# A decoder step on one core: sample state by 32 rows, masked queries against streamed states, and the memory rows of both layers split ahead on VectorE

## The chip, the cores and the metric

The kernel runs on one core of a Trainium2 chip. The time is device microseconds from the first to the last instruction with what the runtime adds around them; the median of several runs counts. The engines are TensorE (PE; its weight loads are shown as PEld), VectorE (DVE), ScalarE (ACT), GpSimd (POOL), and SyncE (SP), which here issues most of the DMAs.

## The reference, cut to what matters

Two layers of a decoder. Layer 0 mixes tokens with HGRN2, a gated linear recurrence with a matrix state of 128 x 128 for each of 8 heads; layer 1 with RWKV-7. Both add a cross attention of 4 heads to a memory of 256 rows, a gate and an output projection. There is one prompt of 1024 tokens from a zero state, and a sample group of 8 sequences with 8 tokens each, which start from given states. What the change touches is the memory's keys and values and the sample group's part of HGRN2:

```python
def memory_kv(mem, g, w):
    kv = rmsnorm(mem, g) @ w
    k, v = jnp.split(kv, 2, axis=-1)
...
    b = jnp.cumsum(gc, axis=2)
    o = jnp.einsum('bhts,bhse->bhte', att, vc) + jnp.einsum('bhtd,bhde->bhte', qc * jnp.exp(b), S)
    b_last = b[:, :, -1:, :]
    S = jnp.exp(b_last[:, :, 0, :])[..., None] * S + jnp.einsum('bhsd,bhse->bhde', kc * jnp.exp(b_last - b), vc)
```

For each head and each of the 8 sequences the output is a product inside the 8 tokens plus decayed queries times the old state; the new state is the decayed old one plus decayed keys times values.

## The kernel before

Everything is fp32. Large products are made of three products of halves: an operand is split into a high part (rounded to fp32r by ACT, "whi", "memh") and a low part (what is left, "wlo", "meml", by POOL or DVE), in `split` (L197 to L200); `mm3` (L216 to L218) adds high x high, high x low and low x high. Small products are plain fp32, and one of them shows as two MATMUL and two weight loads in the trace.

Layer 0 goes through these stages: the tokens are normed and transposed; the values of all heads are made and stored ("vtk"); `memory_kv` makes the memory's keys and values of both layers; then come the eight heads, with the cross attention and the gates as filling between them (the table FILL); then the output projection. Layer 1 follows.

`memory_kv` norms the 256 memory rows once. For each layer it then transposes them on PE (L290), multiplies by the layer's gain on DVE (L291) and splits them into memh and meml, of which there is one buffer each. Eight weight blocks of 128 columns are loaded by SP (L209), split (the low part on POOL for even, on DVE for odd blocks) and multiplied with the rows, 24 matmuls a block; keys and values are transposed back and stored (L311 to L316).

`hgrn_head` makes queries and decays of one head for the 1024 + 64 tokens and calls `hgrn_half` twice; the second call has the sample group's 64 tokens, 8 for each sequence, behind its 512. At its end (from L738 on) it reads the 8 old states of the head in two tiles S0 of four (in the trace, where buffer numbers are left out, S0 is S), and makes

- pi (L744): for each sequence, the state as weights and its 8 queries streamed, which gives the output transposed; ACT copies it to oi (L747);
- pos (L749, L750): the product inside the tokens, plus oi times the identity, which turns it back; then the norm and a transpose into oT;
- kts, the keys transposed (L753, L755), and for each tile of four sequences vx (L758), the values masked by sequence with `blk`, decayed states (L760), the product pds of all 64 keys' rows with vx (L762), the sum (L763) and a store by POOL (L764).

pi, pos, the transposes and pds take turns in two PSUM banks ("z"); vx has one buffer.

The order of the instructions on each engine isn't the program's. The kernel is built with `schedule_with_timeline_sim=True`: a planner plays the program through with times of its own and gives each engine, out of what would be ready, what stands first in the program. So work of different heads, gates and attention is mixed on each engine, and an engine then takes its work strictly in the planned order. Tiles lie in pools that are stacked from both ends of the on-chip memory; with `reuse_waits="tile"` a tile waits only for those tiles that lay at its addresses before.

Of the kernel before, what the change touches and what calls it, by code (L numbers as in the profile page):

```python
# [9 lines left out]
F32 = mybir.dt.float32  # L10
F32R = mybir.dt.float32r
# [43 lines left out]
BF = dict(hs=3, oT=3, qk=3, zn=3, lt=4, kb=2, tot=2, vv=3, cmp=2, kt=1, S=6, oi=1, kts=1, S0=2, vx=1)  # L55
# [94 lines left out]
def pool(g, name, bufs, side="left"):  # L150
    return g.tc.tile_pool(name=name, bufs=bufs, side=side, reuse_waits="tile")
# [117 lines left out]
def memory_kv(g, mp, sp, kT0, v0):  # L269
# [6 lines left out]
    for i in range(2):  # L276
        x = sp("mx")[:, :D]
        nc.sync.dma_start(out=x, in_=g.mem_prompt[0, 128 * i:128 * i + 128, :])
        norm_rows(g, xs[i], x, 128)
    for layer in range(2):  # L280
        mh = mp.tile([128, KT, MEM], F32R, name="memh", tag="memh", bufs=1)
        ml = mp.tile([128, KT, MEM], F32R, name="meml", tag="meml", bufs=1)
        gb = g.vec[:, g.vo["mg"] + layer * KT:g.vo["mg"] + (layer + 1) * KT]
        for i in range(2):
            h = sp("mx")[:, :D].rearrange("p (k t) -> p k t", t=128)
            for b in range(2):
                ps = g.psm.tile([128, 4, 128], F32, name="pt", tag="m")
                for j in range(4):
                    k = 4 * b + j
                    nc.tensor.transpose(ps[:, j, :], xs[i][:, 128 * k:128 * k + 128], g.ident)  # L290
                nc.vector.tensor_tensor(h[:, 4 * b:4 * b + 4], ps, gb[:, 4 * b:4 * b + 4, None].to_broadcast([128, 4, 128]),  # L291
                                        op=ALU.mult)
            sl = (slice(None), slice(None), slice(128 * i, 128 * i + 128))
            split(g, mh[sl], ml[sl], h)
# [6 lines left out]
        for j in range(8):  # L301
            w = load_w(g, mp, g.w_mem_kv[layer, :, 128 * j:128 * j + 128], 128, elo="dve" if j % 2 else "pool", raws=3)
# [128 lines left out]
def hgrn_masks(g, c):  # L431
    nc = g.nc
    si = c.tile([128, 32], I32, name="si")
    ti = c.tile([128, 32], I32, name="ti")
    xi = c.tile([128, 32], I32, name="xi")
# [4 lines left out]
    a = c.tile([128, 32], F32, name="ma")  # L440
    b = c.tile([128, 32], F32, name="mb")
    u = c.tile([128, 32], F32, name="mu_")
# [5 lines left out]
    for n, h in enumerate((2, 4, 8, 16)):  # L448
# [3 lines left out]
        nc.vector.tensor_mul(lev[:, n, :], a, u)  # L452
    return base, lev
# [17 lines left out]
def hgrn_layer(ctx, g):  # L471
# [29 lines left out]
    with pool(g, "xk", 1, "right") as xk:  # L501
# [7 lines left out]
        with pool(g, "hm", 1, "right") as hm, pool(g, "h2", 1, "right") as h2, pool(g, "xc", 1, "right") as xc, \  # L509
# [3 lines left out]
            mbase, mlev = hgrn_masks(g, hm)  # L513
# [107 lines left out]
def hgrn_half(g, hd, half, h2, own, mbase, mlev, qk, zn, lt, vv, att, atts, oT, S):  # L621
# [115 lines left out]
    pi = g.ph["z"].tile([128, TS], F32, name="pi", tag="m")  # L737
    S0 = []  # L738
    for j in range(2):
        s0 = mt("S0", 4, 128)  # L740
        nc.sync.dma_start(out=s0, in_=g.state_hgrn[0, 4 * j:4 * j + 4, hd].rearrange("b d e -> d b e"))
        for b in range(4):
            o = LS * (4 * j + b)
            nc.tensor.matmul(pi[:, o:o + LS], s0[:, b, :], qe[:, 512 + o:512 + o + LS], start=True, stop=True)  # L744
# [4 lines left out]
    nc.tensor.matmul(po[:, 0, :], atts, vv[:64, 4], start=True, stop=False)  # L749
    nc.tensor.matmul(po[:, 0, :], oi, g.ident, start=False, stop=True)  # L750
# [5 lines left out]
    for j, s0 in enumerate(S0):  # L756
        vx = mt("vx", 4, 128, p=64)
        nc.vector.tensor_tensor(vx, vv[:64, 4:5].to_broadcast([64, 4, 128]),  # L758
                                g.blk[:64, 4 * j:4 * j + 4, None].to_broadcast([64, 4, 128]), op=ALU.mult)
        nc.vector.tensor_tensor(s0, s0, ebs[:, 4 * j:4 * j + 4, None].to_broadcast([128, 4, 128]), op=ALU.mult)  # L760
        pd = g.ph["z"].tile([128, 4, 128], F32, name="pds", tag="m")
        nc.tensor.matmul(pd, kt, vx, start=True, stop=True)  # L762
# [1090 lines left out]
```

## Time and profile before

| | |
|---|---|
| median of 3 runs | 2398.97 us (2397.93 to 2401.8) |
| the profiled execution | 2401.76 us, its span 2399.8 us |
| PE busy | 2238.2 us, 93% of the span |
| DVE, ACT, POOL busy | 1332.2, 1004.3, 717.7 us |
| mean clock granted to PE | 0.934 of full speed |

In a row of the windows stand the stretch, its length, for each engine the busy time and in brackets the number of instructions, then the clock granted to PE (1.00 is full speed), the busy share of the DMA engines and GB/s. In a row of the timeline stand the start, the time that it took, the engine, the line, the operation, output and input, shapes and count, and in square brackets how long the engine stood idle before it and for what. Matmuls are pipelined, so the distance of two starts, not the duration of one, is what a matmul costs. In a row of groups stand the count, the busy time in us, the mean of one in ns, and the idle time ahead.

### The profile page before, as it was taken

The numbers are of one execution on the slowest core, as the hardware profiler recorded it, in microseconds if no ns is written. First come the engines' busy times: TensorE is split into PE (matmuls) and PEld (weight loads), VectorE is DVE, ScalarE is ACT, GpSimd is POOL, SyncE is SP. The second block draws the span as 40 slices with busy tenths as digits, with TensorE's granted clock in tenths as the row PEclk, the third lists the DMA queues.
The fourth block names the chain that finished last, engine by engine and source line by source line (L and its number), as shares of the span: only waits on it lengthen the run. The fifth ranks groups of instructions, "written<-read, shape, count | busy, mean of one in ns | idle before, by whom it ended". The sixth has DMA issues, their size and how long they took to land. (4 is left out here: it accounts for less than half of the span.)

```text
span 2399.8 us, 50625 instructions
## 1 busy us (share of the span) xinstructions
PE 2238.2 (93%) x20980; PEld 2001.5 (83%) x20981; DVE 1332.2 (56%) x2678; ACT 1004.3 (42%) x2240; POOL 717.7 (30%) x559
## 2 busy tenths in 40 slices
PE   5988999999999979989989998999999998899997
PEld 5988888888788858878979998898889987788786
DVE  6113566556775553365796214245576589874643
ACT  4222444444444442266554313344544455444421
POOL 2123121122112310034553412113143255444432
PEclk9998999999999989999999998999986798887999
DMA  5334111223432264215434425145332233312653
GB/s 184 86 96 142 48 56 45 67 70 91 111 87 87 80 193 127 84 41 199 148 122 163 127 93 145 50 103 134 113 108 72 57 101 99 90 55 82 201 158 105
DMA packets 360312, 252.99 MB, mean 105 GB/s; under 512 B 120379, under 2 KB 326403, under 8 KB 360083
## 3 DMA queue, kind: packets, MB, share of 16 engines
q1 hardware_dynamic: 348034, 237.66, 33.3%
q0 software_dynamic: 2544, 7.64, 0.9%
q10 hardware_dynamic: 9504, 4.46, 0.7%
q8 instruction: 165, 2.70, 0.5%
q14 instruction: 65, 0.52, 0.1%
HBM read 172.59 MB, written 77.11 MB: 104 GB/s over the span
## 5 line engine op out<-in xcount | busy, mean ns | idle before, releaser
L200 POOL TENSOR_TENSOR wlo<-wraw,whi 128x1024 fp32r<-128x1024 f32 (+1 forms) x84 | 214.9, 2560 | 646.5 <-ACT whi L197 623.8
L216 PE MATMUL pg<-hi,whi 128*128 128x288 f32 (+3 forms) x800 | 269.1, 336 | 4.5 <-DVE qk L597 2.3
L218 PE MATMUL pg<-hi,wlo 128*128 128x288 f32 (+3 forms) x800 | 266.0, 333 | 0.0
L217 PE MATMUL pg<-lo,whi 128*128 128x288 f32 (+3 forms) x800 | 265.9, 332 | 0.0
L197 ACT ACTIVATE whi<-wraw 128x1024 fp32r<-128x1024 f32 (+1 forms) x92 | 101.0, 1099 | 178.5 <-issue 104.9
L216 PEld LDWEIGHTS pg<-hi,whi 128*128 128x128 f32 x800 | 153.8, 192 | 21.5 <-issue 4.4
L217 PEld LDWEIGHTS pg<-lo,whi 128*128 128x128 f32 x800 | 153.7, 192 | 12.9 <-issue 3.1
L218 PEld LDWEIGHTS pg<-hi,wlo 128*128 128x128 f32 x800 | 153.5, 192 | 11.8 <-issue 2.3
L890 PE MATMUL pout<-owh,bh 128*128 128x512 f32 (+1 forms) x432 | 143.1, 397 | 9.2 <-ACT owh L197 9.2
L890 PE MATMUL pout<-owl,bh 128*128 128x512 f32 (+1 forms) x432 | 142.0, 394 | 0.1
L890 PE MATMUL pout<-owh,bl 128*128 128x512 f32 (+1 forms) x432 | 141.2, 394 | 0.9 <-DVE bl L200 0.9
L216 PE MATMUL pg<-xhi,whi 128*128 128x384 f32 (+2 forms) x392 | 127.6, 325 | 7.1 <-DVE evs L1136 5.0
L218 PE MATMUL pg<-xhi,wlo 128*128 128x384 f32 (+2 forms) x392 | 126.4, 322 | 0.0
L217 PE MATMUL pg<-xlo,whi 128*128 128x384 f32 (+2 forms) x392 | 125.5, 320 | 0.0
L1461 PE MATMUL psc<-AR,BKz 128*128 128x128 f32 x544 | 98.2, 342 | 17.2 <-DVE Q L1464 9.3
L1461 PEld LDWEIGHTS psc<-AR,BKz 128*128 128x128 f32 x544 | 86.7, 244 | 23.1 <-DVE Q L1464 11.0
L890 PEld LDWEIGHTS pout<-owh,bh 128*128 128x128 f32 (+1 forms) x432 | 78.9, 183 | 31.3 <-ACT owh L197 10.8
L197 ACT ACTIVATE bh<-br 128x512 fp32r<-128x512 f32 (+1 forms) x54 | 32.4, 606 | 171.5 <-POOL br L859 84.4
L200 DVE TENSOR_TENSOR bl<-br,bh 128x512 fp32r<-128x512 f32 (+1 forms) x54 | 49.6, 919 | 96.2 <-ACT bh L197 96.2
L890 PEld LDWEIGHTS pout<-owh,bl 128*128 128x128 f32 (+1 forms) x432 | 78.6, 182 | 22.8 <-DVE bl L200 1.8
L242 PE MATMUL pg<-xhi,wlo 128*128 128x384 f32 (+1 forms) x408 | 96.6, 334 | 0.0
L890 PEld LDWEIGHTS pout<-owl,bh 128*128 128x128 f32 (+1 forms) x432 | 78.8, 183 | 21.1 <-DVE owl L200 0.6
(460 smaller groups left out, 6114.9 us busy)
## 6 DMA issues: line engine op xcount, KB each, us to landing
wraw<-in_w_in_dram SPq DMA_DIRECT2D x72, 512.0 KB
oraw<-in_w_out_dram SPq DMA_DIRECT2D x24, 512.0 KB
wraw<-in_w_mem_kv_dram SPq DMA_DIRECT2D x16, 512.0 KB
gT<-evs SPq DMA_DIRECT2D x12, 544.0 KB
vv<-vtk SPq DMA_DIRECT2D x24, 256.0 KB
br<-brT SPq DMA_DIRECT2D x24, 256.0 KB
br<-mixT SPq DMA_DIRECT2D x24, 256.0 KB
gt<-gT SPq DMA_DIRECT2D x24, 256.0 KB
```

The costliest lines, as they stand in the source:

```text
L197: nc.scalar.activation(hi, src, AF.Copy)
L200: (nc.gpsimd if elo == "pool" else nc.vector).tensor_sub(lo, src, hi.bitcast(F32))
L216: nc.tensor.matmul(out, ah, bh, start=first, stop=False)
L217: nc.tensor.matmul(out, ah, bl, start=False, stop=False)
L218: nc.tensor.matmul(out, al, bh, start=False, stop=last)
L242: nc.tensor.matmul(z[:, :n], a[:, k], x(k)[:, t0:t0 + n], start=first, stop=last)
L890: nc.tensor.matmul(ps[c][:p], a[:, k, :p], w[:, 512 * c:512 * c + 512], start=first, stop=last)
L1461: nc.tensor.matmul(ps[:, j], two(BK[:, h, j, 2 * e:2 * e + 2]), two(AR[:, j, 2 * e:2 * e + 2]), start=True, stop=True)
```

## The change

In `memory_kv` a first loop over the two layers makes the transposes, the gain and the split for both, with two buffers each for memh and meml, the low parts on DVE; a second loop makes the products, with the low parts of all weights on DVE.

In `hgrn_half` the 64 queries are copied four times, each copy masked to one sequence in four ("qm", with a new mask `cmask` that `hgrn_masks` makes). The output of the old states is then made in place: for each of the four sequences of a tile, 32 masked queries are the weights and the state is streamed (128 columns), added onto 32 rows of pos; the first tile gives rows 0 to 31, the second rows 32 to 63. pi, oi, ACT's copy and the product with the identity go. For the new states the values are masked once for all 64 rows, four ways (with `bmask`, row modulo 32), and each tile's product takes 32 rows of keys and of vx; both products are made ahead of the decays and sums. The pool of masks moves to the left side, and its temporaries to a pool of their own that closes at once.

```diff
-BF = dict(..., S=6, oi=1, kts=1, S0=2, vx=1)
+BF = dict(..., S=6, qm=1, kts=1, S0=2, vx=1)
...
+    ops = []
     for layer in range(2):
-        mh = mp.tile([128, KT, MEM], F32R, name="memh", tag="memh", bufs=1)
-        ml = mp.tile([128, KT, MEM], F32R, name="meml", tag="meml", bufs=1)
+        mh = mp.tile([128, KT, MEM], F32R, name="memh", tag="memh", bufs=2)
+        ml = mp.tile([128, KT, MEM], F32R, name="meml", tag="meml", bufs=2)
...
-            split(g, mh[sl], ml[sl], h)
+            split(g, mh[sl], ml[sl], h, elo="dve")
+        ops.append((mh, ml))
+    for layer in range(2):
+        mh, ml = ops[layer]
...
-            w = load_w(..., 128, elo="dve" if j % 2 else "pool", raws=3)
+            w = load_w(..., 128, elo="dve", raws=3)
...
+    ci, cb = (tmp.tile([128, 4, 64], I32, name=nm) for nm in ("ci", "cb"))
+    nc.gpsimd.iota(ci, pattern=[[0, 4], [1, 64]], base=0, channel_multiplier=0)
+    nc.gpsimd.iota(cb, pattern=[[1, 4], [0, 64]], base=0, channel_multiplier=0)
+    nc.vector.tensor_scalar(ci, ci, 31, 3, op0=ALU.bitwise_and, op1=ALU.logical_shift_right)
+    g.cmask = c.tile([128, 4, 64], F32, name="cmask")
+    nc.vector.tensor_tensor(g.cmask, ci, cb, op=ALU.is_equal)
...
-        with pool(g, "hm", 1, "right") as hm, pool(g, "h2", 1, "right") as h2, ...
+        hm = es.enter_context(pool(g, "hm", 1))
+        with pool(g, "hmt", 1, "right") as tmp:
+            mbase, mlev = hgrn_masks(g, hm, tmp)
+        with pool(g, "h2", 1, "right") as h2, ...
...
-    pi = g.ph["z"].tile([128, TS], F32, name="pi", tag="m")
-    S0 = []
+    qm = mt("qm", 4, TS)
+    nc.vector.tensor_tensor(qm, qe[:, None, 512:].to_broadcast([128, 4, TS]), g.cmask, op=ALU.mult)
+    po = g.ph["z"].tile([64, 1, 128], F32, name="pos", tag="m")
+    nc.tensor.matmul(po[:, 0, :], atts, vv[:64, 4], start=True, stop=False)
+    S0, rs = [], [slice(32 * j, 32 * j + 32) for j in range(2)]
     for j in range(2):
         s0 = mt("S0", 4, 128)
         nc.sync.dma_start(out=s0, in_=g.state_hgrn[...])
-        for b in range(4):
-            o = LS * (4 * j + b)
-            nc.tensor.matmul(pi[:, o:o + LS], s0[:, b, :], qe[:, 512 + o:512 + o + LS], start=True, stop=True)
         S0.append(s0)
-    oi = mt("oi", TS)
-    nc.scalar.activation(oi, pi, AF.Copy)
-    po = g.ph["z"].tile([64, 1, 128], F32, name="pos", tag="m")
-    nc.tensor.matmul(po[:, 0, :], atts, vv[:64, 4], start=True, stop=False)
-    nc.tensor.matmul(po[:, 0, :], oi, g.ident, start=False, stop=True)
+    for b in range(4):
+        for r, s0 in zip(rs, S0):
+            nc.tensor.matmul(po[r, 0, :], qm[:, b, r], s0[:, b, :], start=False, stop=b == 3)
...
-    for j, s0 in enumerate(S0):
-        vx = mt("vx", 4, 128, p=64)
-        nc.vector.tensor_tensor(vx, vv[:64, 4:5].to_broadcast([64, 4, 128]),
-                                g.blk[:64, 4 * j:4 * j + 4, None].to_broadcast([64, 4, 128]), op=ALU.mult)
+    vx = mt("vx", 4, 128, p=64)
+    nc.vector.tensor_tensor(vx, vv[:64, 4:5].to_broadcast([64, 4, 128]),
+                            g.bmask[:64, :4, None].to_broadcast([64, 4, 128]), op=ALU.mult)
+    pds = [g.ph["z"].tile([128, 4, 128], F32, name="pds", tag="m") for _ in range(2)]
+    for r, pd in zip(rs, pds):
+        nc.tensor.matmul(pd, kt[r], vx[r], start=True, stop=True)
+    for j, (s0, pd) in enumerate(zip(S0, pds)):
         nc.vector.tensor_tensor(s0, s0, ebs[:, 4 * j:4 * j + 4, None]..., op=ALU.mult)
-        pd = g.ph["z"].tile([128, 4, 128], F32, name="pds", tag="m")
-        nc.tensor.matmul(pd, kt, vx, start=True, stop=True)
         nc.vector.tensor_add(s0, s0, pd)
```

More of the change, by code (lines that the diff above doesn't have):

```diff
@@ L54 @@
 RB1 = dict(s=5, AR=6, Q=6, BKt=5, BKts=2, UV=3, UVs=2, XN=1, XP=1, W=3, S0=2, S1=2, yv=3, o4=3, ec=6, ecs=2, Sn0=2)
-BF = dict(hs=3, oT=3, qk=3, zn=3, lt=4, kb=2, tot=2, vv=3, cmp=2, kt=1, S=6, oi=1, kts=1, S0=2, vx=1)
+BF = dict(hs=3, oT=3, qk=3, zn=3, lt=4, kb=2, tot=2, vv=3, cmp=2, kt=1, S=6, qm=1, kts=1, S0=2, vx=1)
 QW = 640
@@ L301, in memory_kv @@
         for j in range(8):
-            w = load_w(g, mp, g.w_mem_kv[layer, :, 128 * j:128 * j + 128], 128, elo="dve" if j % 2 else "pool", raws=3)
+            w = load_w(g, mp, g.w_mem_kv[layer, :, 128 * j:128 * j + 128], 128, elo="dve", raws=3)
             dst = kT[:, j, :] if j < 4 else vT[:, j - 4, :]
@@ L428, in sample, with hgrn_masks @@
             nc.sync.dma_start(out=g.mixT[D:, TP:].rearrange("(h c) t -> c h t", c=128), in_=self.os)
-def hgrn_masks(g, c):
+def hgrn_masks(g, c, tmp):
     nc = g.nc
-    si = c.tile([128, 32], I32, name="si")
-    ti = c.tile([128, 32], I32, name="ti")
-    xi = c.tile([128, 32], I32, name="xi")
+    si = tmp.tile([128, 32], I32, name="si")
+    ti = tmp.tile([128, 32], I32, name="ti")
+    xi = tmp.tile([128, 32], I32, name="xi")
     nc.gpsimd.iota(si, pattern=[[0, 32]], base=0, channel_multiplier=1)
@@ L439, in hgrn_masks @@
     nc.vector.tensor_tensor(xi, si, ti, op=ALU.bitwise_xor)
-    a = c.tile([128, 32], F32, name="ma")
-    b = c.tile([128, 32], F32, name="mb")
-    u = c.tile([128, 32], F32, name="mu_")
+    a = tmp.tile([128, 32], F32, name="ma")
+    b = tmp.tile([128, 32], F32, name="mb")
+    u = tmp.tile([128, 32], F32, name="mu_")
     nc.vector.tensor_tensor(u, ti, si, op=ALU.is_ge)
@@ L508, in hgrn_layer @@
         g.ph = {k: ph.get(k, ph["o"]) for k in "loz"}
-        with pool(g, "hm", 1, "right") as hm, pool(g, "h2", 1, "right") as h2, pool(g, "xc", 1, "right") as xc, \
+        hm = es.enter_context(pool(g, "hm", 1))
+        with pool(g, "hmt", 1, "right") as tmp:
+            mbase, mlev = hgrn_masks(g, hm, tmp)
+        with pool(g, "h2", 1, "right") as h2, pool(g, "xc", 1, "right") as xc, \
                 pool(g, "hq", 1, "right") as hq, pool(g, "hs", BF["hs"], "right") as hs:
@@ L512, in hgrn_layer @@
             hslot = lambda nm, b=0: hs.tile([128, 1024], F32, name=nm, tag="s")
-            mbase, mlev = hgrn_masks(g, hm)
             att = [hm.tile([128, 4, 128], F32, name=f"att{j}") for j in range(2)]
```

## The prediction

> **What bounds the kernel now.** I read the table of windows first, to see which engine fills which stage, then the timeline of PE where it isn't full.
>
> ```profile
> span 2399.8 us, 50625 instructions
> ...
> core 0: us, PE busy (x) PEld busy (x) DVE busy (x) ACT busy (x) POOL busy (x), PEclk, DMA share, GB/s
> 149.00:225.00 76.00, 61.00 (x448) 58.02 (x446) 20.86 (x26) 25.85 (x37) 31.79 (x20) 0.87 0.48 140
> 260.00:845.00 585.00, 577.21 (x6208) 490.04 (x6207) 363.95 (x930) 266.61 (x658) 122.35 (x97) 0.98 0.26 75
> 1620.00:2230.00 610.00, 573.58 (x8153) 524.21 (x8151) 415.23 (x796) 285.21 (x700) 253.93 (x256) 0.84 0.34 92
> ```
>
> The memory stage (149 to 225) has PE idle for 15 of 76 us and a clock of 0.87. The heads (260 to 845) have PE busy for 577.2 of 585 us at a clock of 0.98, while DVE, the next engine, has 364. So in the heads time taken off PE is time taken off the span, and in the memory stage PE's gaps have to be looked at.
>
> ```profile
> 149.05 1.91 PE L290 MATMUL pt<-ident,mxs 128*128 128x128 f32 x16
> 156.09 0.58 PE L216 MATMUL pg<-memh,whi 128*128 128x256 f32 x1 [5.13 <-ACT whi L197]
> ...
> 160.38 0.58 PE L218 MATMUL pg<-memh,wlo 128*128 128x256 f32 x1 [1.55 <-DVE wlo L200]
> ...
> 189.26 0.27 PE L290 MATMUL pt<-ident,mxs 128*128 128x128 f32 x1
> ...
> 192.62 0.80 PE L216 MATMUL pg<-memh,whi 128*128 128x256 f32 x2 [1.45 <-ACT memh L197]
> 196.98 0.58 PE L217 MATMUL pg<-meml,whi 128*128 128x256 f32 x1 [3.57 <-POOL meml L200]
> ...
> 202.43 0.28 PE L216 MATMUL pg<-memh,whi 128*128 128x256 f32 x1
> 202.55 0.28 PE L217 MATMUL pg<-meml,whi 128*128 128x256 f32 x1
> ...
> 189.30:202.40 13.10, 7.11 (x34) 6.34 (x32) 3.11 (x4) 3.49 (x5) 5.91 (x5) 0.61 0.38 120
> ```
>
> There are two gaps. The first opens when the transposes of layer 0's memory rows end, and PE waits for the first weights: for their high part till 156.09, for a low part till 160.38. The second stands between the layers: memh and meml exist once, so layer 1's rows can be split only after layer 0's last product, and PE waits for memh (ACT) and then for meml (POOL). The clock granted in the second is 0.61, since the idle time slows what follows.
>
> **Memory, second gap.** From 189.26 to 202.43 are 13.2 us, and they hold 34 matmuls. At the full pitch of 0.12 us (202.43 to 202.55) these need 4.1 us, so the gap with its slow clock costs 9.1 us. With two buffers each, layer 1's memh and meml are ready some 30 us earlier, and the products of layer 1 follow those of layer 0; what is late next there is the weights, whose path (load, ACT, split) already keeps step inside a layer. I take 9.0 off.
>
> **Memory, what moves to the front.** The 16 transposes of layer 1 go from among the products to the first gap. Sixteen of them are 1.91 us at 149.05, a pitch of 0.11, so 1.8 us leave a stretch where PE is full, and the new place lies inside PE's idle 5.13 us. With them go four mults by the gain, and all meml and all weight splits go from POOL to DVE:
>
> ```profile
> L291 DVE TENSOR_TENSOR mx<-pt,vec 128x512 f32<-128x512 f32 x8 | 5.1, 684 | 71.9 <-PE pt L290 71.9
> ...
> L200 DVE TENSOR_TENSOR wlo<-wraw,whi 128x1024 fp32r<-128x1024 f32 x8 | 11.0, 1380 | 41.5 <-ACT whi L197 41.5
> ...
> L200 POOL TENSOR_TENSOR meml<-mx,memh 128x1024 fp32r<-128x1024 f32 x4 | 9.4, 2350 | 49.8 <-ACT memh L197 49.8
> ```
>
> DVE gets 8 more weight splits and 4 rows of meml, 12 x 1.38 = 16.6 us, on top of its 20.9 in this stage: 37 of some 65 us, so it isn't the bound. A layer's product of 24 matmuls takes 24 x 0.12 = 2.9 us and its weight split 1.4, so the splits keep pace, and a low part is there 1 us sooner than from POOL (2.35 for the same shape). The question is the order on DVE in the first gap. If the planner puts all of layer 1's rows ahead of the first weight split, DVE has 8 x 0.68 + 4 x 1.38 + 1.38 = 12.3 us to do from about 149.5 on (four transposes after 149.05), and the first low weights come at 161.8 instead of 160.38, with those of the next product 1.4 us behind: up to 2 us lost. If the split of the weights goes between them, it ends at about 157.5 (PE starts on the high part at 156.09, and 1.38 behind that): 3 us won. I take zero, and keep +2 and -3.
>
> **Masks and addresses.** The batch mask adds two DVE operations of 256 elements and two iotas to the masks, which end just ahead of the first evacuation of head 0:
>
> ```profile
> 232.05 0.20 DVE L452 TENSOR_TENSOR mlev<-ma,mu__2183 128x32 int32<-128x32 f32 x1
> 232.16 0.68 DVE L157 TENSOR_SCALAR qk<-pg 128x512 f32<-128x512 f32 x1
> ...
> 236.50 0.61 PE L216 MATMUL pg<-hi,whi 128*128 128x288 f32 x1 [2.34 <-DVE qk L597]
> ```
>
> That evacuation starts as soon as DVE is through with the masks, and PE waits for what follows from it. At 0.68 for 512 elements, two of 256 are about 0.8 us, and nothing hides them unless they go behind the evacuation: +0.8, between 0 and +2 (the memory slots that the new place of the masks lies under come free late). The larger memory pool also pushes the slots of the head stage under those of the memory, by the sizes in the code (a partition has xk 10 KB, mem 44 and then 60, ms 34, so the memory ends at 88 KB and then at 104; the head stage's slots lay from 92 KB on and will lie from 87). The cached keys of the first sample batches, now loaded early, then wait for the end of the memory stage:
>
> ```profile
> 69.27 2.42 SPq L396 DMA_DIRECT2D kc<-in_cache_mem_k_dram  x5
> ...
> 227.83 0.61 SPq L316 DMA_DIRECT2D kv<-v  x1
> 244.96 0.37 SPq L209 DMA_DIRECT2D wraw<-in_w_in_dram  x1
> ```
>
> One such issue takes 0.48 us, two batches have 32, so 15.5 us on SP's queue, and the queue has 16.5 us with nothing to issue between 227.83 and 244.96. I count zero; without that cover the weight loads behind them come late, at most +6.
>
> **Sample state, the products.** What one head does now and the nearest rows for what it will do:
>
> ```profile
> 449.18 1.95 PE L744 MATMUL pi<-qk,S 128*128 128x8 f32 x16
> 451.06 0.43 PE L749 MATMUL pos<-vv,atts 64*64 64x128 f32 x2
> ...
> 826.36 0.43 PE L750 MATMUL pos<-ident,oi 128*64 128x128 f32 x2
> 826.73 0.40 PE L216 MATMUL pg<-hi,whi 128*128 128x288 f32 x1
> ...
> 596.59 0.64 PE L415 MATMUL pos<-vc,PTs 128*32 128x128 f32 x15
> 597.16 0.40 PE L217 MATMUL pg<-lo,whi 128*128 128x288 f32 x1
> ...
> 308.99 0.45 PE L694 MATMUL plev<-qk 128*32 128x32 f32 x16
> 309.37 0.66 PE L350 MATMUL ppt<-ident,prob 128*128 128x128 f32 x4
> ...
> 325.22 0.45 PE L648 MATMUL plev<-qk 128*32 128x32 f32 x28
> 325.59 0.49 PE L730 MATMUL po<-S,qk 128*128 128x128 f32 x2
> ```
>
> Removed: the pi products, 1.88 us from start to start (16 matmuls of 0.118, though each streams 8 columns: it is the state as weights that costs), and the product of oi with the identity, 0.37. Added: 16 matmuls that stream 128 columns of the state past weights of 32 columns, in two column strips in turn. The same shape in four strips is L415, 15 in 0.57 us, 0.038 each. How two strips stand to four, L694 and L648 show with 32 columns: 0.38/16 = 0.024 against 0.37/28 = 0.013, 1.8 times. So 0.068 each, 1.10 us a head. Bounds: 0.61 (as fast as four strips) and 1.88 (as slow as full weights). Won a head: 1.88 + 0.37 - 1.10 = 1.15, so 9.2 us for eight, between 3.0 and 13.1. [...]
>
> **Sample state, the update.**
>
> ```profile
> 341.51 1.12 PE L762 MATMUL pds<-vx,kts 64*128 64x512 f32 x2
> 342.56 0.39 PE L216 MATMUL pg<-hi,whi 128*128 128x256 f32 x1
> ...
> L758 DVE TENSOR_TENSOR vx<-vv,blk 64x512 f32<-64x512 f32 x16 | 12.8, 802 | 1.6 <-DMA vv<-vtk 1.6
> ```
>
> Now two products over 64 rows, apart in time, 1.05 us each and about 0.09 for the change of shape ahead: 2.28 a head. After: two over 32 rows each, side by side in the array, into two banks. If they run at once, one block of 1.14; if not, 2.10. No row shows row strips alone; I take 1.6, halfway, as the column strips gained but not fully: 0.68 a head, 5.4 us in all, between 1.4 and 9.1. On DVE one vx in place of two, and a smaller qm: nothing, DVE has the room. The wait that is added: both products need both of the two z banks, and what is queued behind them on PE waits too; but the bank last in use is that of pks, and its evacuation they need anyway.
>
> At the end of the stage the update's tail isn't what the output projection waits for: its weights stand on SP's queue behind a gated row's load, whose store is issued at 862.05. Zero, from -3 to +3.
>
> ```profile
> 862.05 0.33 SPq L535 DMA_DIRECT2D brT<-oT  x1
> ...
> 867.31 1.95 SPq L834 DMA_DIRECT2D oraw<-in_w_out_dram  x4
> ```
>
> **Sum.** -9.0 - 1.8 + 0.8 - 9.2 - 5.4 = -24.6 us. The profiled execution took 2401.8 us (2.0 of it around the span), 2.8 above the median of the runs, 2398.97. So 2377 for it and 2374.4 for the median; I say 2375.
>
> **The rivals.** (1) The strips don't run side by side: 1.88 for the state products, 2.10 for the update, so 4.4 us are won in the heads instead of 14.6: 2385. For it: no row has two column strips with 128 columns, none has row strips. Against: L415. (2) The change doesn't do what it says in the memory stage: the planner keeps layer 1's rows where they were, or they come late behind the weight splits on DVE, and the 10.8 us stay: 2385 or 2386. For it: PE and DVE take their work in the planner's order, and the first gap shows PE held for a split on DVE (160.38). Against: 30 us lie between. (3) Nearly nothing is left: the bad ends of the heads (4.4), the cached keys' loads (+6) and the first gap (+2) together: about 2394. (4) Slower: the clock granted in the second layer falls. There PE is busy for 573.6 of 610 us with small products at a clock of 0.84, where the heads have 0.98; every order there is the planner's, whose simulated times all move. At 0.79 the same work takes 573.6 x (0.84/0.79 - 1) = 36 us more: 2411. It decides from a clock of 0.80 on (29 us). For it: the 0.84 itself, the clock falls easily there. Against: no instruction of that layer is touched.
>
> **How the numbers follow.** Forecast 0.61, rival 1 0.13, rival 2 0.08, rival 3 0.09, rival 4 0.09. A measurement of this kernel can tell about 0.2%, 4.8 us, from no change. Forecast and rivals 1 and 2 are faster (0.81, a little of them lost to the bound), rival 3 the same (0.10), rival 4 slower (0.09). The forecast alone lies from 2362 to 2389; all good ends together give 2358, and the bad end of rival 3 2396: the range.
>
> **What would show it.** After: no wait of PE for memh or meml between the layers, and the last memory product some 11 us earlier (0.9 clock or more over the stage); all wlo and meml of the stage on DVE; 16 matmuls of 32 weight columns in about 1.1 us a head and a pair of update products in 1.1 to 2.1; PE's busy time in the heads less by 10 to 20 us, and the stage shorter by the same. Wrong, if the heads don't get shorter with it, or if the second layer's clock or its length moves by over 10 us.

## The result, and the profile after

The kernel after takes 2356.08 us (median of 4 runs, 2353.59 to 2360.24) against 2398.45 us (4 runs, 2394.4 to 2401.8) of the kernel before: a ratio of 0.9823, interval 0.9803 to 0.9843. That is 42 us less, where 24 were forecast. A later measurement with more runs, below, gives 31 us (0.9871, 0.9835 to 0.9908), and the stages that the change touches account for 36. Over everything that was measured for this document, 64 runs of the kernel before have a median of 2394.4 us and 11 of the kernel after 2359.3: 35 us.

The head of the page of the kernel after, and its table of windows over the stretches that the prediction showed of before:

```profile
span 2352.2 us, 50578 instructions
...
149.00:225.00 76.00, 68.13 (x507) 65.96 (x505) 40.18 (x66) 28.79 (x43) 5.25 (x12) 0.93 0.58 164
260.00:845.00 585.00, 557.47 (x6121) 473.64 (x6120) 381.61 (x946) 276.19 (x669) 124.99 (x103) 0.97 0.30 87
1620.00:2230.00 610.00, 572.79 (x8132) 515.24 (x8131) 423.53 (x818) 294.21 (x716) 267.49 (x264) 0.88 0.37 103
```

The same clock times now hold later work, so these rows only give the manner: in the memory stage POOL's work is nearly gone (31.8 to 5.3 us) and DVE's has doubled, PE is fuller and its clock higher (0.93 for 0.87); and the second layer, which the change does not touch, has a clock of 0.88 where it had 0.84.

To compare like with like I cut the trace at the same instructions: memory, from the start of the first transpose of memory rows to the start of the last product of memh with wlo; heads and tail, from there to the start of the first output product (pout); recurrence, from the first to the last product of layer 1's chain (the tile of that name). All that is left goes under "rest". Microseconds, one profiled execution a row:

| kernel | span | memory | heads and tail | recurrence | rest |
|---|---|---|---|---|---|
| before | 2399.8 | 75.3 | 649.6 | 484.9 | 1190.0 |
| before, again | 2389.8 | 75.0 | 648.6 | 474.3 | 1191.9 |
| after | 2352.2 | 60.9 | 629.2 | 471.1 | 1191.0 |
| after, again | 2357.5 | 60.6 | 625.2 | 484.2 | 1187.5 |
| after, a third | 2350.7 | 61.2 | 628.4 | 469.8 | 1191.3 |

Of the 47.6 us between the first two profiled spans, the memory stage has 14.4, the heads with their tail 20.4, and 13.8 are in the recurrence. The repeats show which of these are of the change: memory is 14.3 us shorter and heads with tail 21.5 each time within a few us, but the recurrence of one and the same program differs by 10 to 14 us between two executions ("again" and "a third" are further executions of the same kernels).

PE's waits in the memory stage, before (line and buffer that waits, who is waited for, us in total, times, longest):

```profile
PE pg L216 <- ACT whi L197: 7.1, 3, 5.1
PE pg L217 <- POOL meml L200: 3.6, 1, 3.6
PE pg L218 <- DVE wlo L200: 1.6, 1, 1.6
PE pg L216 <- ACT memh L197: 1.5, 1, 1.5
PE pt L311 <- ACT vT L305: 1.2, 2, 1.0
```

and after, where the second row belongs to head 0 already:

```profile
PE pg L216 <- ACT whi L197: 4.8, 2, 3.4
PE pg L216 <- DVE qk L610: 2.6, 1, 2.6
PE pg L218 <- DVE wlo L200: 0.3, 1, 0.3
PE pt L315 <- ACT vT L309: 0.3, 1, 0.3
```

15.0 us of waits became 5.4; nothing waits for memh or meml. That is 9.6 of the stage's 14.3 us. The rest is PE's own work, which takes 55.8 us instead of 60.5 in the stage, at a granted clock of 0.94 instead of 0.86. The timeline of PE and one of its windows, after:

```profile
148.53 3.66 PE L291 MATMUL pt<-ident,mxs 128*128 128x128 f32 x32
155.59 0.39 PE L216 MATMUL pg<-memh,whi 128*128 128x256 f32 x1 [3.40 <-ACT whi L197]
157.35 0.58 PE L216 MATMUL pg<-memh,whi 128*128 128x256 f32 x1 [1.38 <-ACT whi L197]
...
158.63 0.58 PE L218 MATMUL pg<-memh,wlo 128*128 128x256 f32 x1 [0.27 <-DVE wlo L200]
```

```profile
158.63:209.50 50.87, 50.87 (x408) 50.87 (x409) 23.46 (x26) 19.01 (x29) 4.15 (x10) 0.95 0.60 177
```

All 32 transposes stand in the first gap, and still the gap is 1.2 us shorter (10.1 from 148.53 to 158.63, against 11.3 from 149.05 to 160.38), and from its end to the last product PE is busy for 50.87 of 50.87 us at a clock of 0.95. The second gap is gone.

One head, PE's timeline after: each block with the row that follows it.

```profile
357.36 1.07 PE L761 MATMUL pos<-S,qm 128*32 128x128 f32 x16
358.36 0.40 PE L217 MATMUL pg<-lo,whi 128*128 128x288 f32 x1
...
325.40 1.13 PE L772 MATMUL pds<-vx,kts 32*128 32x512 f32 x4
326.45 0.39 PE L216 MATMUL pg<-hi,whi 128*128 128x256 f32 x1
...
823.55 2.08 PE L772 MATMUL pds<-vx,kts 32*128 32x512 f32 x4 [0.36 <-ACT kts L766]
838.62 1.97 PE L902 MATMUL pout<-owh,bh 128*64 128x512 f32 x4 [12.99 <-ACT owh L197]
```

The 16 state products take 1.00 us from start to start (1.88 and 0.37 before). The pair of update products, four matmuls, takes 1.05 us: as much as one of the two took before (1.05), so the two row strips run wholly side by side; by the trace's single matmuls, the second strip's starts 7 ns after the first's. The same single matmuls show the state products in two strips as well: in one strip they follow each other at 0.109 us, and the other strip runs beside it 0.03 us behind. The last two rows are the end of the stage, with the pair of the last head (at a granted clock of 0.50 there); the tail's experiment comes back to them.

### The profile page after: what moved, and what is told of

It reads as the page before. It is cut to its first block, busy times and chain, and to the rows that moved or that the text cites. A ratio compares the mean times of both kernels' runs of the same rounds, so it can differ in the third digit from the quotient of the medians.

```text
span 2352.2 us, 50578 instructions
## 1 busy us (share of the span) xinstructions
PE 2191.5 (93%) x20965; PEld 1966.2 (84%) x20965; DVE 1343.7 (57%) x2692; ACT 1002.3 (43%) x2232; POOL 688.7 (29%) x549
## 5 line engine op out<-in xcount | busy, mean ns | idle before, releaser
L200 POOL TENSOR_TENSOR wlo<-wraw,whi 128x1024 fp32r<-128x1024 f32 (+1 forms) x76 | 195.8, 2578 | 583.2 <-ACT whi L197 529.8
L218 PE MATMUL pg<-hi,wlo 128*128 128x288 f32 (+3 forms) x800 | 263.9, 330 | 0.0
L218 PEld LDWEIGHTS pg<-hi,wlo 128*128 128x128 f32 x800 | 151.9, 190 | 11.6 <-issue 2.0
L218 PE MATMUL pg<-xhi,wlo 128*128 128x384 f32 (+2 forms) x392 | 126.1, 322 | 0.0
L1473 PE MATMUL psc<-AR,BKz 128*128 128x128 f32 x544 | 92.0, 324 | 9.6 <-DVE Q L1476 4.8
L242 PE MATMUL pg<-xhi,whi 128*128 128x384 f32 (+1 forms) x408 | 94.9, 331 | 0.0
```

The costliest lines, as they stand in the source:

```text
L200: (nc.gpsimd if elo == "pool" else nc.vector).tensor_sub(lo, src, hi.bitcast(F32))
L218: nc.tensor.matmul(out, al, bh, start=False, stop=last)
L242: nc.tensor.matmul(z[:, :n], a[:, k], x(k)[:, t0:t0 + n], start=first, stop=last)
L1473: nc.tensor.matmul(ps[:, j], two(BK[:, h, j, 2 * e:2 * e + 2]), two(AR[:, j, 2 * e:2 * e + 2]), start=True, stop=True)
```

## Experiments

The theory was that every part gives what its block of instructions on PE shows, that the parts add up, and that the update pair makes most of the difference to the forecast. Its rivals: the parts give what was forecast and the second layer gave the rest, by chance of the execution or by the order that the planner made for it. (Letters in the expectations are those of the expectation in which they stand.) Stages below are those of the table; "before" is 75.2, 649.1 (means of two), "after" 60.9, 627.6 (means of three).

**The kernel before, once more.**

```diff
 (no edit; a second execution under the profiler)
```

> The kernel before once more, unchanged, for one more profile of the same order of instructions. The question is the second layer's recurrence (from the first to the last chain matmul, 485 us before, 471 us after). Theory A, the planner's order makes the 14 us: this profile shows 485 within 3 us again. Theory B, it is the chance of an execution (the granted clock): it comes out anywhere between 470 and 490, with the clock of that stretch moving along.

2391.78 us. Its memory stage and heads repeat to 1 us; its recurrence is 474.3 us instead of 484.9.

**The memory part alone.**

```diff
+        mh = mp.tile(..., name="memh", tag="memh", bufs=2)   # and meml
...
+            split(g, mh[sl], ml[sl], h, elo="dve")
+        ops.append((mh, ml))
+    for layer in range(2):
+        mh, ml = ops[layer]
...
+            w = load_w(..., 128, elo="dve", raws=3)
```

> Only the memory edit: both layers' rows ahead in two buffers, all low parts of the stage on DVE; heads as before. Theory: the stage from the last value product to the last memory product goes from 75.3 to about 61 us, and the total falls by 12 to 16 us. Rival, the gain of the whole is mostly the planner's order elsewhere: the stage shortens as said, but the total moves by something quite different (less than 5 or more than 25 us).

2378.42 us, ratio 0.9930 (0.9904 to 0.9956). The memory stage takes 61.2 us, all of what it takes in the kernel after; heads and tail 647.1, 2 less than before.

**The state products alone** (with the masks they need).

```diff
+    qm = mt("qm", 4, TS)
+    nc.vector.tensor_tensor(qm, qe[:, None, 512:]..., g.cmask, op=ALU.mult)
...
-            nc.tensor.matmul(pi[:, o:o + LS], s0[:, b, :], qe[:, 512 + o:512 + o + LS], start=True, stop=True)
...
-    nc.scalar.activation(oi, pi, AF.Copy)
...
-    nc.tensor.matmul(po[:, 0, :], oi, g.ident, start=False, stop=True)
+    for b in range(4):
+        for r, s0 in zip(rs, S0):
+            nc.tensor.matmul(po[r, 0, :], qm[:, b, r], s0[:, b, :], start=False, stop=b == 3)
```

> Only the state products by masked queries (with the masks' new pools that they need space for); memory and update as before. Theory: 16 products in about 1.0 us a head in place of 1.88 and 0.37, heads shorter by 8 to 12 us, the total by as much. Rival: the gain in the heads came from the update alone, and this gives 0 to 3 us.

2398.66 us, ratio 1.0018 (0.9998 to 1.0039): nothing by the total. By the stages heads and tail take 639.7 us, 9.4 less, and eight times 1.88 + 0.37 - 1.00 are 10.0. The gain is there (with what the masks' move gives or takes, below), and the recurrence of this kernel, 496.8 us, is 12 to 22 longer than those of before; PE stands idle in it for 42.6 us, against 26.7 and 23.4. That was the first sign that totals do not show a small edit here.

**The update pair alone.**

```diff
-    for j, s0 in enumerate(S0):
-        vx = mt("vx", 4, 128, p=64)   # masked by g.blk, once a tile
+    vx = mt("vx", 4, 128, p=64)       # masked by g.bmask, once
...
+    for r, pd in zip(rs, pds):
+        nc.tensor.matmul(pd, kt[r], vx[r], start=True, stop=True)
...
-        nc.tensor.matmul(pd, kt, vx, start=True, stop=True)
```

> Only the update by 32 rows with one vx, both products ahead; memory and state products as before. Theory: a pair in 1.05 us in place of two times 1.14, heads shorter by 9 us and by up to 4 more at the last head, where the second vx was waited for. Rival: the pair takes 2.0 us when it isn't beside the new products, and the gain is 1 to 3 us.

2392.16 us, ratio 0.9982 (0.9962 to 1.0001). Heads and tail 640.8 us, 8.3 less. The 2.28 us of before have 0.09 in them for the change of shape ahead of each of the two products; the pair of 1.05 has such a change ahead of it once, so eight times 2.28 - 1.14, 9.1 us, are to be compared.

**The kernel after, once more.**

```diff
 (no edit; a second execution under the profiler)
```

> The changed kernel once more, unchanged, for a second profile of its order. Second layer's recurrence, first to last chain matmul: theory A (the order makes it): 471 us within 3. Theory B (chance of the execution): it moves by more, with the clock of that stretch.

2359.31 us; memory 60.6, heads and tail 625.2, recurrence 484.2 against 471.1. So the 13.8 us by which the first two profiles differ in the recurrence are no more than two executions of one program differ by.

**The masks and their pools alone** (the batch mask is made, and nothing uses it).

```diff
+        hm = es.enter_context(pool(g, "hm", 1))
+        with pool(g, "hmt", 1, "right") as tmp:
+            mbase, mlev = hgrn_masks(g, hm, tmp)   # with ci, cb, cmask
```

> Only the masks' pools moved (left side, temporaries closed at once) and the batch mask made, which nothing uses here: no product changes. It measures what new addresses and a new planned order do by themselves. Theory: within 5 us of before. Rival: the order alone is worth more than 8 us, either way, and then the sum of the parts needn't be the whole.

2382.16 us, ratio 0.9964 (0.9941 to 0.9988). Heads and tail 645.3 us, 3.8 less, not 0.8 more. The kernel of the state products has this move in it too, so its 9.4 us are not those of the products alone.

**Update products over 64 rows.** The kernel after, but each tile's product takes all 64 rows again, with keys that are zero in the other half; so no row strips, and in the program still both products one behind the other.

```diff
-    nc.scalar.activation(kt, pk, AF.Copy)
+    for j in range(2):
+        nc.scalar.activation(kts[j], pk, AF.Copy, scale=g.half[:64, j:j + 1])
...
-        nc.tensor.matmul(pd, kt[r], vx[r], start=True, stop=True)
+        nc.tensor.matmul(pd, kt, vx, start=True, stop=True)
```

(The tiles of state have five buffers instead of six, for room.)

> The changed kernel, but the two update products go over all 64 rows, with keys whose other half is zero (one more small copy on ACT a head, one state buffer less); one vx and both products ahead as in the change. Theory, the two strips of 32 rows run at once: here the pair takes 2.0 us instead of 1.05 and the total is 7 to 9 us longer than the changed kernel. Rival, what paid was that the products stand together and ahead: no longer than the changed kernel within 3 us.

PE's timeline of this kernel, a pair that stands together:

```profile
396.75 1.98 PE L776 MATMUL pds<-vx,kts 64*128 64x512 f32 x4
398.67 0.40 PE L217 MATMUL pg<-lo,whi 128*128 128x288 f32 x1
```

1.92 us for the pair against 1.05: without row strips one product runs behind the other. In five of the heads the planner put other work between the two, which then take 1.05 each. For the seven heads ahead of the last, two as shown and five with a second change of shape, that is 2 x 0.87 + 5 x 1.14 = 7.4 us. Heads and tail are 12 longer than the mean of after (639.5), so some 5 more were lost, to the second copy on ACT, the fifth buffer or the order, which was not traced further. The total, 2350.27 us (0.9811, 0.9778 to 0.9844), was nevertheless no longer than that of the kernel after: its recurrence took 452.3 us. The last runs come back to this.

**State products without alternation.** The kernel after, but in the program the four products of rows 0 to 31 stand ahead of the four of rows 32 to 63.

```diff
-    for b in range(4):
-        for r, s0 in zip(rs, S0):
+    for r, s0 in zip(rs, S0):
+        for b in range(4):
```

> The changed kernel, but the state products of the first strip all stand ahead of those of the second, so that strips don't alternate. Theory, alternating strips overlap: the block of 16 goes from 1.0 to about 1.85 us a head, 7 us longer in all. Rival, the small weights (32 columns to load instead of 128) are what pays: still about 1.0 us a head, and no change of the total beyond 3 us.

2351.89 us, ratio 0.9830 (0.9801 to 0.9859). PE's timeline of this kernel:

```profile
510.20 1.51 PE L761 MATMUL pos<-S,qm 128*32 128x128 f32 x16
511.64 0.70 PE L359 MATMUL pxo<-PT,v 128*128 128x256 f32 x2
```

1.44 us for 16 instead of 1.00, and not the 1.85 of the theory. The single matmuls say why: the second strip does not stand wholly behind the first. In each strip the eight matmuls follow each other at 0.109 us, but the second strip's first starts with the first strip's fifth (0.45 us after its first), so four of the eight run side by side; whether the planner or the engine put them so, the trace doesn't say. Counted in steps of 0.109 us, with 0.13 to the row behind, the block is 12 steps here (1.44) and 8 with alternation (1.00); with nothing side by side it would be 16, 1.87 us by this estimate, which is what the 16 products with 128 weight columns took before (1.88). So weights of 32 columns by themselves gain nothing: all of the 0.88 us comes from two strips that run side by side, and the rival is out. For eight heads the order of the loops is worth 3.5 us; heads and tail are 2.9 longer than the mean of after (630.5), which fits, though one program differs by 4 there.

**The memory part's two halves.** First the buffers and the order, with the low parts left on POOL (meml) and on POOL and DVE in turn (weights):

```diff
+        mh = mp.tile(..., name="memh", tag="memh", bufs=2)   # and meml
...
+        ops.append((mh, ml))
+    for layer in range(2):
+        mh, ml = ops[layer]
```

> The kernel before with the memory part alone, and of that only the order: two buffers each of memh and meml, both layers' rows split ahead of the products; the low parts stay where they were (meml on POOL, the weights' low parts on POOL and DVE in turn). Theory A (the buffers close the gap between the layers, the splits on DVE are worth little): the stage takes 61 to 64 us instead of 75.3, PE has no wait for memh or meml after the first product. Rival B (both edits are needed: with the low parts on POOL the products wait for them at every second weight, as POOL takes 2.35 us for one against 1.38): 66 to 70 us. In total 2378 to 2386, of which the second layer can take 10 either way.

Then the low parts on DVE, with one buffer and layer 1's rows split after layer 0's products:

```diff
-            split(g, mh[sl], ml[sl], h)
+            split(g, mh[sl], ml[sl], h, elo="dve")
...
-            w = load_w(..., 128, elo="dve" if j % 2 else "pool", raws=3)
+            w = load_w(..., 128, elo="dve", raws=3)
```

> The kernel before with the other half of the memory part alone: all low parts of the stage on DVE, one buffer, and layer 1's rows split after layer 0's products as before. Theory A: the gap between the layers stays and is shorter by what DVE is faster than POOL for the last low part of the rows (2.35 - 1.22 = 1.1 us, perhaps twice): the stage takes 71 to 74 us instead of 75.3. Rival B (the low parts on POOL are what the gap is made of): under 68. The two halves should add up to the 14 us of the whole.

The memory stage takes 64.0 us with the first (2389.14 us in all, 0.9967, 0.9946 to 0.9988) and 67.0 with the second (2378.72 us, 0.9925, 0.9896 to 0.9955), 75.2 without and 60.9 with both. PE's waits with the buffers alone, and with DVE alone:

```profile
PE pg L216 <- ACT whi L197: 4.5, 3, 3.3
PE pg L216 <- DVE qk L601: 2.3, 1, 2.3
PE pg L218 <- DVE wlo L200: 1.6, 1, 1.6
PE pg L217 <- POOL meml L200: 0.6, 1, 0.6
```

```profile
PE pg L216 <- ACT whi L197: 5.1, 1, 5.1
PE pg L217 <- DVE meml L200: 1.8, 1, 1.8
PE pg L216 <- ACT memh L197: 1.5, 1, 1.5
PE pt L311 <- ACT vT L305: 1.2, 2, 1.0
PE pg L218 <- DVE wlo L200: 0.5, 1, 0.5
```

For the buffers the theory holds, at the edge of its range: no wait between the layers, 11.2 us, where 10.8 were worked out. For DVE the rival holds: I had expected 71 to 74. The gap between the layers stays but its wait for meml is halved (3.6 to 1.8), and in the first layer the waits for weights fall (wlo 1.6 to 0.5; of whi, 2.0 beyond the first 5.1 to nothing). These waits are 4.9 of the 8.2 us; the rest is PE's work at a clock of 0.91 instead of 0.87 (149 to 226). The halves sum to 19.4 and together give 14.3: both shorten the same gap, and what DVE adds once the gap is closed is 3.1 us.

**The last head's store by another queue.** The prediction left the tail at zero; by the trace it has a length of its own. SP's queue after, and then one row of ACT:

```profile
824.47 0.33 SPq L548 DMA_DIRECT2D brT<-oT  x1
825.71 0.36 SPq L867 DMA_DIRECT2D br<-brT  x1
826.12 1.92 SPq L846 DMA_DIRECT2D oraw<-in_w_out_dram  x4
828.14 10.59 SPq L867 DMA_DIRECT2D br<-brT  x3
```

```profile
836.99 0.63 ACT L197 ACTIVATE bh<-br 128x512 fp32r<-128x512 f32 x1 [8.57 <-DMA br<-brT]
```

ACT takes its work in the planned order, so the output weights' split stands behind this row, at 837.53, and PE waits for it (the 12.99 above, 9.24 before). From the store of the last gated row (824.47) to the first output product (838.62) are 14.15 us; before, from 862.05 to 873.94, 11.89. In the kernel with the edit POOL's queue issues the last head's two stores:

```diff
-GQ = ()
+GQ = (7,)
 ...
     (nc.gpsimd if j in GQ else nc.sync).dma_start(out=g.brT[128 * j:128 * j + 128, ...], in_=m[...])
```

> The kernel after with one edit: the last head's gated rows are stored by POOL's DMA queue instead of SP's, where the store stands ahead of the output projection's weight loads. Theory A (the output projection waits for the gated row's load, and that for the store: SP's queue is held by it): the tail from the last update product to the first output product is 9 to 11 us instead of 14, the total 3 to 5 us less. Rival B: the load waits for the same multiplication and the same store wherever it is issued: 14 us again, total within 2 us.

POOL's queue and PE in this kernel:

```profile
820.46 0.58 POOL L548 DMA_DIRECT2D brT<-oT  x1 [0.30 <-POOL oT L545]
```

```profile
819.16 2.08 PE L772 MATMUL pds<-vx,kts 32*128 32x512 f32 x4 [0.36 <-ACT kts L766]
829.49 1.97 PE L902 MATMUL pout<-owh,bh 128*64 128x512 f32 x4 [8.26 <-ACT owh L197]
```

9.0 us from store to output product instead of 14.15, so the tail depends on where the store and the loads behind it are queued: theory A, for the stage. Heads and tail take 620.3 us, 7 less than after. But the total was 2366.69 us (0.9880, 0.9844 to 0.9917), 10.6 more than the first measurement of after and not 3 to 5 less: its recurrence took 492.7 us.

**Order or chance in the second layer.** The kernel with 64 rows once more; then this, the kernel after and the one with the moved store, measured side by side on one chip.

```diff
 (no edit in any of the four against the kernels above)
```

> The kernel with the update products over 64 rows once more, without a change, for a second execution under the profiler. Its second layer's recurrence took 452.3 us, where ten other profiles have 471 to 497. Theory A (its planned order is better, the clock follows): 450 to 456 again. Rival B (chance of the execution, as the kernels before and after showed with 10 and 13 us between two executions each): anywhere from 452 to 485.

> The kernel after, timed again beside the next two on one chip. By stages it is 36 us shorter than the kernel before; in the first measurement the total was 42 less. Theory B (the 6 us are chance, as the recurrence of the second layer differs by 10 to 17 us between executions of one program): a ratio of 0.983 to 0.987. Theory A (the planned order of the second layer, which is new in every kernel, is a little better here): 0.980 to 0.983 again.

> The kernel with the last head's gated rows stored by POOL's queue. Its stages ahead of the second layer are 5 us shorter than those of the kernel after. Theory A (the length of the second layer belongs to a program's planned order): the total stays 8 to 12 us above that of the kernel after, as the first measurements had it (2366.7 against 2356.1), and the recurrence takes 488 us or more. Theory B (chance of the execution): 3 to 6 us below the kernel after, and a recurrence of 470 to 485.

> The kernel with the update products over 64 rows. Its heads are 13 to 17 us longer than those of the kernel after, its tail 2 us shorter. Theory A (planned order): the total is nevertheless the same as that of the kernel after or less, within 5 us, since its recurrence is shorter by 10 us or more. Theory B (chance): 10 to 16 us above the kernel after.

Before took 2392.54 us there; after 2361.6 (0.9871, 0.9835 to 0.9908), the moved store 2369.11 (0.9907, 0.9875 to 0.9939), 64 rows 2359.72 (0.9854, 0.9816 to 0.9892). One execution of the last kernel by itself, between the two measurements, took 2361.6, with a recurrence of 469.5 where the first had 452.3: chance, rival B. By the stages ahead of the second layer the moved store should be 7 us faster than after and 64 rows 13 slower (641.1 in the mean of its three profiles). They are 7.5 slower and 2 faster, which is what theory A says for the totals of both. After's own ratio, 0.9871, lies at the edge of its theory B. The recurrence of the moved store is 493.4 us, as theory A asks; that of 64 rows is 7 shorter than that of after beside it (462.5 against 469.8), where theory A asked for 10. Windows over the recurrence (length, then PE's busy time first, the clock third from the end) of before, of two executions of after, of the moved store, and of two executions of 64 rows:

```profile
1744.40:2229.30 484.90, 458.16 (x7034) 416.07 (x7030) 346.14 (x659) 226.72 (x567) 221.88 (x227) 0.81 0.31 85
```

```profile
1713.10:2184.20 471.10, 443.75 (x7056) 402.30 (x7054) 348.19 (x671) 229.73 (x579) 227.06 (x230) 0.85 0.33 89
```

```profile
1703.20:2187.40 484.20, 453.88 (x7058) 412.24 (x7055) 348.73 (x673) 230.05 (x579) 227.90 (x232) 0.83 0.32 87
```

```profile
1701.70:2195.10 493.40, 445.45 (x7051) 402.20 (x7050) 354.86 (x663) 228.37 (x575) 225.44 (x229) 0.82 0.31 84
```

```profile
1717.50:2169.80 452.30, 430.73 (x7032) 388.32 (x7031) 346.05 (x660) 227.11 (x567) 224.25 (x227) 0.87 0.34 91
```

```profile
1724.00:2193.50 469.50, 444.99 (x7032) 401.69 (x7031) 345.53 (x660) 227.24 (x567) 226.80 (x228) 0.84 0.33 88
```

Take PE's busy time from the length. PE's idle time is 26.7 and 23.4 us in the two profiles of before, 27.4, 30.3 and 26.6 in the three of after, 48.5 and 48.0 with the moved store, 21.6, 24.5 and 26.4 with 64 rows: it belongs to the program, and it repeats within 5 us. PE's busy time for the same products goes with the clock and differs inside one program: 443.3 to 453.9 us after, 430.7 to 445.0 with 64 rows, at 0.85 and 0.83, 0.87 and 0.84. So both theories have their part. The planner makes a new order of the second layer with every edit of the first: in the traces DVE's and ACT's instructions of the recurrence come in one and the same order in every execution of a program (but for two instructions at the edge of the stretch), and in another order in every other program. For the moved store this order is worth up to 21 us of PE's waits (48 against 27), and the kernels with the state products alone (42.6) and with the memory's buffers alone (44.8), profiled once each, are of its kind. The clock differs between executions of one program, by 7 to 14 us of PE's busy time. But it is not all chance: over whole runs it is 0.938 to 0.944 in the ten of the moved store and 0.944 to 0.954 in the eleven of 64 rows. Why a program's clock lies higher was not found. So the moved store is explained by PE's waits; 64 rows only in small part, since its idle time is some 4 us less than that of after (24 against 28 in the mean of three), and most of what makes up for its longer heads is a higher clock.

For the kernel after the order is no better than before (27 to 30 against 23 to 27 us idle); its three recurrences have a mean of 475.0 us, before's two 479.6, which does not tell them apart. The gain that is shown for the change is therefore the 36 us of its own stages, and 31 and 42 us are two readings of it with the second layer's differences on top. In the total the row strips of the update show nothing: without them the kernel took 2350.27 and 2359.72 us, with them 2356.08 and 2361.6.

## Why the prediction was right or wrong

The direction and the forecast's case were right: the mechanisms that the forecast counted on are in the traces, and none of its rivals came about. The size was not: 24.6 us were summed where the stages have 35.8. The first measurement, 2356.08, lies 1.9 us under the range's lower end of 2358, the second, 2361.6, inside the range. These 5.5 us between two measurements of one kernel are no property of the change; the sum was too small by 11 us either way. Two terms failed, by nearly the same amount: the update pair (5.4 us for 9.1) and the low parts on DVE (nothing for some 3.5). By its steps:

- *Memory, second gap and transposes, 10.8 us.* Right. The buffers and the order alone gave 11.2, and what was to show it did: no wait for memh or meml between the layers. The slow clock that the gap was charged with is in the trace of before: behind the wait of 3.57 us the matmuls follow each other at 0.21 us, from 197.36 to 202.27, at a granted clock of 0.50, and from 202.43 on at 0.12, at 1.00.
- *Low parts on DVE, zero, between +2 and -3.* This step failed: the good end was right, and the choice of the middle wasn't. The prediction itself gave the case: if the weights' split goes between the rows' splits, 3 us are won. L218 starts at 158.63, the first gap is 1.2 us shorter, and with the second gap closed by the buffers DVE is worth 3.1 us (64.0 to 60.9); 14.3 less the 10.8 that were worked out leaves 3.5. Which of the two orders the planner would take was not worked out, and the middle of the two is neither.
- *Masks, +0.8.* Not found. PE's wait for head 0's first queries is 2.6 us, as before (2.3): the planner put the two mask operations into time in which DVE was idle. The masks alone took 3.8 us off heads and tail, which is no more than the 4 us by which heads and tail of one program differ between executions; so not even its sign is sure.
- *Cached keys' loads on SP, zero.* Right, with the wait that was named: after, SP issues them from 215.88 on,

```profile
211.87 0.34 SPq L320 DMA_DIRECT2D kv<-v  x1
215.88 6.66 SPq L400 DMA_DIRECT2D kc<-in_cache_mem_k_dram  x13
...
232.81 0.40 SPq L209 DMA_DIRECT2D wraw<-in_w_in_dram  x1
```

  where before they went out from 69.27 on; they moved as the pools' sizes said, and SP's empty time covered them.
- *State products, 9.2 us (1.10 us a head).* Right, with some luck: 1.00 a head, 10.0 us in all, 9.4 in heads and tail for the edit alone, masks included. That the strips run side by side is what the forecast counted on; the way from four strips to two by the rows of plev, which stream 32 columns and not 128, came out close. What the block consists of are 8 steps of 0.109 us and 0.13 to the next row. The sum left out that the two blocks that go had a change of shape ahead, 0.126 us each behind the products of plev, where the new one has 0.012: another 1.9 us in eight heads, by an estimate from these rows. And "it is the state as weights that costs" is not borne out: with the state streamed, a matmul inside one strip takes 0.109 us, about what it took as weights (0.118). In a strip the weights for the next matmul start to load 2 ns after the one before has started, over all 128 rows like it, and take 0.11 us.
- *Update pair, 5.4 us (1.6 us a pair).* This step failed: the mechanism was right, the size was off by 3.7 us. The pair takes 1.05 and a change of shape ahead, so 1.14, the good bound, and 9.1 us. I took the middle of the bounds "as the column strips gained but not fully". The likeness does not bear the middle: the ratio that I had read from the column strips was 1.8, which makes 2.28 / 1.8 = 1.27 a pair, not 1.6; and the column strips of the state products, too, run side by side throughout. The second row strip starts 7 ns after the first, and the pair takes 1.05 us, against 1.92 over 64 rows.
- *Tail, zero, between -3 and +3.* Right in its reason, that the output projection does not wait for the update: in the last head the update's second product waited for vx before (the third row is the output projection's first product),

```profile
859.91 1.12 PE L762 MATMUL pds<-vx,kts 64*128 64x512 f32 x2 [0.45 <-ACT kts L755]
862.62 2.07 PE L762 MATMUL pds<-vx,kts 64*128 64x512 f32 x2 [1.59 <-DVE vx L758]
873.94 1.97 PE L890 MATMUL pout<-owh,bh 128*64 128x512 f32 x4 [9.24 <-ACT owh L197]
```

  These are 4.8 us from the first row's start to the second's end, against 2.1 after; and these 2.7 us are not gained, since the stage ends with the store and its load. From the store on it is 2.3 us longer (14.15 against 11.89), inside the range that was given; why the store takes longer to come back was not traced.
- *Second layer, untouched; rival 4 at 0.09.* The rival's mechanism exists, though not as priced: a new order is worth up to 21 us by PE's waits, in the kernel with the moved store, while the clock differs between executions of one program and between programs. For this change the waits came out at nothing, and the clock did not fall. The prediction's own sign of a failure, "the second layer's clock or its length moves by over 10 us", was met by the first two profiles (13.8 us, 0.84 to 0.88 in the window) and says nothing, because one program does the same by itself. For the same reason the 0.2% that the prediction took as the bound of a measurement was too fine: two measurements of the same pair of kernels gave 42 and 31 us.

Summed again with what was measured: memory 14.3, and in heads and tail state products 10.0, their changes of shape 1.9, update 9.1, the way from the last store -2.3, and 2.8 that no part accounts for, together 21.5: 35.8 us, or 2363 from the median shown before. The remaining 7 to the first measurement are what the second layer gives or takes; the kernel before, too, came out at 2398.45 there, 4 us above the median of all its runs. The lower end of the range was not its own sum either: the good ends of the terms (first gap 3, masks 0.8, state products 3.9, update 3.7, tail 3) are 14.4 us, which gives 2360 and not 2358.

## What to carry to other kernels

When two bounds lie far apart, take the ratio that the nearest row gives (here 1.8 of 2 from the column strips) and not the middle between them; and where two orders are possible, work out which one the planner takes, since the middle of the two is a time that neither gives. Read an experiment's single matmuls before its block time: 1.44 us looked like a half gain of narrow weights and was a half overlap of two strips. Where a planner orders the whole program, read an edit in its own stage, cut at the same instructions in both traces: the state products were worth 9.4 us in their stage and nothing in the total. And profile the kernel before twice, since without the second execution the 14 us of the second layer would have been put down to the change.

## What the runs showed of the hardware

- Two products over 32 rows each, 512 columns streamed, into two banks, take the time of one: 1.05 us for four matmuls, against 1.92 over 64 rows.
- In one column strip, fp32 matmuls with 32 weight columns and 128 streamed follow each other at 0.109 us, against 0.118 with 128 weight columns and 8 streamed (16 in 1.88 us). Two strips run beside each other: 16 in 1.00 us.
- In a strip the weights for the next matmul start to load 2 ns after the one before has started (0.11 us for 32 columns); both use all 128 rows.
- In one stretch of small products, the granted clock differs between executions of one program (0.81 to 0.82, 0.83 to 0.85, 0.84 to 0.87), and PE's busy time of some 440 us by 7 to 14 us with it.
- From the store of the last gated row to the first output product, with the load that reads it back and a split on ACT between, went 14.15 us with the store on SP's queue, and 9.0 us with it on POOL's.
